# A two-block transformer layer on one core: the first bias strip loaded earlier, the embedding's product by token halves, two silus pinned behind copies

## The chip, the cores and the metric

The kernel runs on one core of a Trainium2 chip. The metric is the device time of one execution in microseconds. Five engines work side by side, each through its own instructions in order: TensorE (PE in the profile, with PEld for its weight loads), VectorE (DVE), ScalarE (ACT), GpSimd (POOL), and SyncE (SP), which here issues the DMAs.

## The reference, cut to what matters

Two transformer blocks over 1024 tokens of width 1024. The change lies in the second block:

```
y_mla  = mla_group(...)        # latent attention, 8 heads: softmax(q k^T) v
y_diff = diff_group(...)       # differential attention, 4 heads, two maps each
x = x + concat(y_mla, y_diff) @ w_out
x = x + conv_ffn(rms_norm(x))  # (silu(conv(h @ w_gate)) * (h @ w_up)) @ w_down
gate = sigmoid(rms_norm(x) @ w_ple_gate)
x = x + gate * (p @ w_ple_proj)

# diff_group, per block of 128 queries
bias   = table[t5_bucket(k_idx - q_idx)]
logits = q k^T * scale + bias, masked by chunks; probs = softmax(logits)
attn   = probs[map 0] - lam * probs[map 1];  lam from lambda_q1, k1, q2, k2
```

## The kernel before

Every fp32 product is made of three products of fp32r halves: a tensor is split into a high part and the rest (names ending in h and l; the weights' halves are both called hl). Weights are loaded as `raw`, then split on ScalarE or GpSimd.

The order of the instructions on each engine is set by a scheduler when the program is built: it goes by its own estimate of when data is ready, and by the order in which the code traces the work. `tc.keep_in_program_order(i)` pins an instruction behind the instruction of the same engine that was traced just before it. Memory is given out in pools that are opened and closed like a stack, on a left and a right side; a tile that falls on a closed pool's memory waits for the readers of what lay there. `bufs` is the number of copies of a tile.

The second block runs like this. `mla()` is the latent attention's loop over head pairs and query blocks. Between its steps `mix` puts pieces of another generator, the fill: `diff_proj()` (the projections of the differential attention), then `ahead()` (its first loads), then `ple_proj()`, the embedding's product p @ w_ple_proj. Then `diff()` is the main loop, with `out2a()` (the first part of the output projection, tiles `mix00` to `mix13`, added into `x`) as its fill.

`ple_proj` transposes nothing: pT, the embedding by columns, is loaded as `p_raw` and split into pT0h, pT0l (tokens 0 to 511) and pT1h, pT1l (512 to 1023). It makes 16 units, one for each of 4 weight groups and 4 token pairs, of 12 matmuls each. A unit's result is copied from PSUM by two ScalarE copies into `p_o` (two buffers) and each is stored to DRAM (`dr_pp`).

`diff()` needs for each head a strip of bias, 128x1024 fp32, loaded from DRAM (`dr_f`) in a skewed view, with one corner set by a GpSimd memset. VectorE adds strip and logits and takes the row's maximum in one instruction (L1341, shown as ISA in the order, CUSTOM_DVE_ANT_0 in the trace), ScalarE takes the exponential, and VectorE joins the two maps with `nlam`, which comes from the small tile `lam` (`lam_p`, `lam_s`).

The feed-forward part, `ffn()`, makes 11 pairs of products: the gate's, and the gated one (h @ w_up) that is multiplied by silu(conv(gate)). Each is made by `wino()`, a two by two block scheme with seven products of 12 matmuls instead of eight, in this order on TensorE: B11, B21, T2, T1, T3, T4, B22 (names of the activations' blocks). Four PSUM tiles are used: x takes B11, T2 and T3 one on top of the other, with copies `u1`, `u2`, `u3` of its state taken by ScalarE (L1571, tile `w_u`) before the next product adds to it; z takes B21, y takes T1 and then B22, q takes T4. In the gated product VectorE adds a copy to a PSUM tile into `f_c` (one buffer, L1621), then multiplies it into `f_y`, silu's output (L1622). It does so in the order z with u1 into the first rows of `ys[0]`, y with u3 into `ys[1]`, q with u3 into `ys[1]`, y with u2 into `ys[0]`. B22 adds to y, so it can't start before the second of these sums has read y. The gated product issues `silu(ys[1])` when u2 is traced, `silu(ys[0])` when u3 is.

Of the kernel before, what the change touches and what calls it, by code (L numbers as in the profile page):

```python
# [11 lines left out]
F32 = mybir.dt.float32  # L12
# [3 lines left out]
AF = mybir.ActivationFunctionType  # L16
ALU = mybir.AluOpType
# [8 lines left out]
NEG = -1e30  # L26
# [138 lines left out]
class Kern:  # L165
# [1099 lines left out]
    def ahead(self):  # L1265

        self.fp_close()
        self.xn2b_close()
        self.qp, self.qp_close = self.open("dfq")
        self.qk0 = self.load_qk(self.qp, self.dr_dqk[0], 0)  # L1270
        yield 0.0

    def diff(self):
        nc, d, tc, vec = self.nc, self.d, self.tc, self.vec
# [5 lines left out]
        sp = es.enter_context(self.pool("df", 1, "right"))  # L1280
# [16 lines left out]
        st, strip = {}, {}  # L1297

        def values(hd, half):
            v = sp.tile([128, 4, 128], F32, tag=f"v{half}", name="v", bufs=2 - half)  # L1300
            nc.sync.dma_start(v, self.dr_dv[:, 4 * half:4 * half + 4, hd * 128:hd * 128 + 128])
            return v

        def first(hd):
            qk = [self.load_qk(qp, self.dr_dqk[hd], 0) if hd else self.qk0]
            o = sp.tile([128, NT, 128], F32, tag="o", name="o", bufs=2)
            skew = self.dr_f[hd][0:1, 127:128]
            strip[hd] = sp.tile([128, 1024], F32, tag="strip", name="strip", bufs=2)
            nc.sync.dma_start(strip[hd], bass.AP(tensor=skew.tensor, offset=skew.offset, ap=[[1152, 128], [1, 1024]]))

            nc.gpsimd.memset(strip[hd][0:64, 960:1024], NEG)
            v = [values(hd, 0)]
            st[hd] = qk, v, o, sp.tile([128, NT], F32, tag="o_ss", name="o_ss", bufs=2)

        def s0(hd, i):
            if i == 0:
                if hd == 0:
                    first(hd)
# [4 lines left out]
            if i == 4 and hd < 3:  # L1323
                first(hd + 1)
# [112 lines left out]
    def ple_proj(self):  # L1437

        nc, d = self.nc, self.d
        with self.pool("pp") as fp:  # L1440
            pT = [self.pair(fp, f"pT{h}", 2) for h in range(2)]
            for h in range(2):
                for k in range(2):
                    pr = fp.tile([128, 512], F32, tag="p_raw", name="p_raw", bufs=1)
                    nc.sync.dma_start(pr, d["pT"][:, k, h * 512:h * 512 + 512])
                    nc.scalar.copy(pT[h][0][:, k], pr)
                    nc.gpsimd.tensor_tensor(pT[h][1][:, k], pr, pT[h][0][:, k].bitcast(F32), ALU.subtract)
            for gi in range(4):
                w = self.W(d["w_pp"][gi])
                for tp in range(4):  # L1450
                    ps = self.tm(w, pT, 2, tp)
                    for j in range(2):
                        o = fp.tile([128, 256], F32, tag="p_o", name="p_o", bufs=2)
                        nc.scalar.copy(o, ps[:, j])
                        nc.sync.dma_start(self.dr_pp[gi, tp, :, j], o)
                    yield 0.25

    def mix_late(self):

# [72 lines left out]
    def wino(self, src, pool, out, ahead=400, then={}):  # L1532
# [5 lines left out]
        with self.tc.high_priority(offset=ahead):  # L1538
            for k in range(2):
                raw = self.wraw.tile([128, 1056], F32, tag="raw", name="raw")[:, :1024].rearrange("p (f n) -> p f n", f=2)  # L1540
                nc.sync.dma_start(raw, src[:, k].rearrange("p f k n -> p f (k n)"))
                raws.append(raw)
            (a11, a21), (a12, a22) = ((r[:, 0], r[:, 1]) for r in raws)

            def split(v):
                hl = self.whl.tile([128, 2, 528], F32R, tag="hl", name="hl")[:, :, :512]
                nc.scalar.copy(hl[:, 0], v)  # L1547
                nc.gpsimd.tensor_tensor(hl[:, 1], v, hl[:, 0].bitcast(F32), ALU.subtract)  # L1548
                return [(hl[:, 0, k * 128:k * 128 + 128], hl[:, 1, k * 128:k * 128 + 128]) for k in range(4)]

            def add(a, b, op):
                v = self.wsum.tile([128, 512], F32, tag="w_s", name="w_s")
                nc.gpsimd.tensor_tensor(v, a, b, op)
                return v
            w1, w2 = split(a11), split(a12)
            s1 = add(a21, a22, ALU.add)
            s2 = add(s1, a11, ALU.subtract)
            w6, w5 = split(s2), split(s1)
            w7 = split(add(a11, a21, ALU.subtract))
            w4 = split(a22)  # L1560
            w3 = split(add(a12, s2, ALU.subtract))
# [30 lines left out]
    def ffn(self):  # L1592

        nc, d, tc, vec = self.nc, self.d, self.tc, self.vec
        with self.pool("ffn", 1) as fp:
            for gi in range(11):
                us = []
                for _ in range(2):
                    u = fp.tile([128, 2 + T], F32, tag="f_u", name="f_u", bufs=2)
                    nc.vector.memset(u[:, 0:2], 0.0)  # L1600
                    us.append(u)

                def gate(ct, half, ps, v):
                    u = us[ct][:, 2 + half * 512:514 + half * 512]
                    nc.vector.tensor_tensor(u, ps, v, ALU.add)  # L1605
                self.wino(d["w_fg"][gi], fp, gate)
                cw = vec["cw2"]
                ys = {}
                for ct in (1, 0):
                    c, u = 2 * gi + ct, us[ct]  # L1610
                    y = fp.tile([128, T], F32, tag="f_y", name="f_y", bufs=2)
                    nc.vector.tensor_scalar(y, u[:, 0:T], cw[:, c, 0:1], vec["cb2"][:, c:c + 1], ALU.mult, ALU.add)  # L1612
                    for j in range(1, 3):
                        nc.vector.scalar_tensor_tensor(y, u[:, j:j + T], cw[:, c, j:j + 1], y, ALU.mult, ALU.add)  # L1614
                    ys[ct] = y
                silu = lambda y: nc.scalar.activation(y, y, AF.Silu)

                def up(ct, half, ps, v):
                    y = ys[ct][:, half * 512:half * 512 + 512]
                    c = fp.tile([128, 512], F32, tag="f_c", name="f_c", bufs=1)  # L1620
                    nc.vector.tensor_tensor(c, ps, v, ALU.add)  # L1621
                    nc.vector.tensor_tensor(y, y, c, ALU.mult)  # L1622
                self.wino(d["w_fu"][gi], fp, up, 400 if gi else 100,
                          {"u2": lambda: silu(ys[1]), "u3": lambda: silu(ys[0])})
                for ct in range(2):
                    nc.sync.dma_start(self.dr_h[2 * gi + ct], ys[ct])
        self.xb_close()
        self.xt_close()
        self.ws_close()
        self.xa_close()  # L1630
# [90 lines left out]
```

## Time and profile before

| what | us |
|---|---|
| median of 3 runs | 2645.79 |
| lowest and highest run | 2638.98, 2645.89 |
| time of the profiled execution | 2637.64 |
| span of the profiled execution | 2635.9 |
| PE busy | 2490.2 (94%) |
| DVE busy | 1435.8 (54%) |
| POOL busy | 1054.8 (40%) |
| ACT busy | 869.3 (33%) |

All times inside the execution count from the span's start. The profiled execution is 8.15 below the median and 1.34 below the lowest of the three runs; its own time is 1.7 over its span. TensorE is busy for most of the span; what it waits for is what a change can win or lose. The mean granted clock of TensorE was 0.982 of full speed.

### The profile page before, as it was taken

What the parts mean: (1) busy time and instruction counts of PE and PEld (TensorE: products, weight loads), DVE (VectorE), ACT (ScalarE), POOL (GpSimd) and SP (SyncE); (2) the same over time, 40 slices, a digit from 0 to 9 for tenths busy, and PEclk for the clock granted to TensorE, in tenths of its full rate; (3) what the DMA queues carried; (4) which work ended last, traced back from release to release, by engine and by line L of the source; (5) the groups of instructions that cost most, each with busy time, mean ns of one, the idle gap of its engine ahead of it and who ended that gap; (6) DMA issues with size and microseconds to landing.
All of it is one profiled execution on the core that took longest, in us unless ns stands there. A gap on an engine that the chain in (4) does not pass through costs nothing.

```text
span 2635.9 us, 38621 instructions
## 1 busy us (share of the span) xinstructions
PE 2490.2 (94%) x15170; PEld 2119.0 (80%) x15170; DVE 1435.8 (54%) x2677; ACT 869.3 (33%) x1599; POOL 1054.8 (40%) x914
## 2 busy tenths in 40 slices
PE   6999999999999999998899989988999999999999
PEld 6888999876777779988787868887777777777789
DVE  5565555275666553368854338846544544433372
ACT  3322223163444341123334346624333333100030
POOL 1524332122122245544533322224777777533322
PEclk9999999999999999999999999989999999999999
DMA  4433223253422455322675457451222122523222
GB/s 163 141 110 112 81 89 105 65 151 97 116 84 69 167 177 180 115 72 90 203 214 167 120 186 205 136 188 58 67 92 80 64 89 87 185 79 104 72 85 93
DMA packets 158766, 313.55 MB, mean 119 GB/s; under 512 B 14804, under 2 KB 62164, under 8 KB 158456
## 3 DMA queue, kind: packets, MB, share of 16 engines
q1 hardware_dynamic: 158584, 311.07, 37.8%
q8 instruction: 120, 1.97, 0.3%
q14 instruction: 62, 0.51, 0.1%
HBM read 214.01 MB, written 100.42 MB: 119 GB/s over the span
## 4 chain that ended last, share of the span: by engine, by line
PE 40%; DVE 9%; DMA 3%; issue 2%; ACT 2%; POOL 1%; SPq 0%; ACTq 0%; DVEq 0%; POOLq 0%
PE pj L1567 13%; PE pj L266 6%; PE pj L264 6%; PE pj L265 6%; DVE f_y L1614 1%; PE po L932 1%; PE pt L925 1%; PE po L1367 1%; DVE f_y L1612 1%; PE z L1337 1%; PE z L264 1%; DVE rs_a L304 1%; PE z L265 1%; PE z L266 1%; DMA f_y<-dr_h 1%
## 5 line engine op out<-in xcount | busy, mean ns | idle before, releaser
L255 POOL TENSOR_SCALAR hl<-raw 128x512 fp32r<-128x512 f32 (+2 forms) x262 | 192.7, 740 | 897.4 <-PE pj L266 884.1
L256 POOL TENSOR_TENSOR hl<-raw,hl 128x512 fp32r<-128x512 f32 (+3 forms) x270 | 367.7, 1369 | 34.0 <-ACT hl L253 17.9
L265 PE MATMUL pj<-hl,xn_0h 128*128 128x256 f32 (+2 forms) x544 | 159.0, 292 | 2.7 <-POOL hl L256 2.7
L264 PE MATMUL pj<-hl,xn_0h 128*128 128x256 f32 (+2 forms) x544 | 160.4, 295 | 0.6 <-DVE qb_st L314 0.6
L264 PE MATMUL pj<-hl,xn_1h 128*128 128x256 f32 (+2 forms) x544 | 159.6, 293 | 0.0
L266 PE MATMUL pj<-hl,xn_0l 128*128 128x256 f32 (+2 forms) x544 | 159.3, 293 | 0.0
L265 PE MATMUL pj<-hl,xn_1h 128*128 128x256 f32 (+2 forms) x544 | 157.3, 289 | 0.0
L266 PE MATMUL pj<-hl,xn_1l 128*128 128x256 f32 (+2 forms) x544 | 157.2, 289 | 0.0
L1548 POOL TENSOR_TENSOR hl<-w_s,hl 128x512 fp32r<-128x512 f32 x88 | 117.6, 1341 | 66.9 <-ACT hl L1547 66.7
L266 PE MATMUL pj<-hl,f_hl 128*128 128x512 f32 x352 | 139.8, 399 | 2.3 <-DVE f_hl L1653 2.3
L264 PE MATMUL pj<-hl,f_hh 128*128 128x512 f32 x352 | 139.7, 397 | 2.0 <-DVE xres L1662 1.6
L1548 POOL TENSOR_TENSOR hl<-raw,hl 128x512 fp32r<-128x512 f32 x66 | 103.1, 1568 | 91.5 <-ACT hl L1547 91.5
L265 PE MATMUL pj<-hl,f_hh 128*128 128x512 f32 x352 | 138.9, 395 | 0.0
L1662 DVE TENSOR_TENSOR xres<-xres,pj 128x512 f32<-128x512 f32 x96 | 65.2, 686 | 129.9 <-PE pj L266 118.2
L264 PE MATMUL pj<-xn_0h,hl 128*128 128x512 f32 x288 | 117.6, 408 | 0.0
L264 PE MATMUL pj<-xn_1h,hl 128*128 128x512 f32 x288 | 116.6, 405 | 0.0
L927 DVE COPY aT<-pt 128x512 f32<-128x512 f32 (+1 forms) x112 | 70.6, 630 | 83.6 <-PE pt L925 83.4
L265 PE MATMUL pj<-xn_1l,hl 128*128 128x512 f32 x288 | 116.1, 403 | 0.0
L266 PE MATMUL pj<-xn_0h,hl 128*128 128x512 f32 x288 | 115.1, 400 | 0.0
L265 PE MATMUL pj<-xn_0l,hl 128*128 128x512 f32 x288 | 114.8, 398 | 0.0
L266 PE MATMUL pj<-xn_1h,hl 128*128 128x512 f32 x288 | 114.4, 397 | 0.0
L1605 DVE TENSOR_TENSOR f_u<-pj,w_u 128x512 f32<-128x512 f32 x44 | 30.3, 689 | 148.6 <-ACT w_u L1571 96.5
(595 smaller groups left out, 7316.9 us busy)
## 6 DMA issues: line engine op xcount, KB each, us to landing
raw<-in_w_o_dram SPq DMA_DIRECT2D x28, 512.0 KB
qk<-dr_mla SPq DMA_DIRECT2D x32, 416.0 KB
dr_mla<-l_st SPq DMA_DIRECT2D x32, 384.0 KB
raw<-in_w_fg_dram SPq DMA_DIRECT2D x22, 512.0 KB
raw<-in_w_fu_dram SPq DMA_DIRECT2D x22, 512.0 KB
dr_h<-f_y SPq DMA_DIRECT2D x22, 512.0 KB
raw<-in_w_fd_dram SPq DMA_DIRECT2D x22, 512.0 KB
f_y<-dr_h SPq DMA_DIRECT2D x22, 512.0 KB
```

What stands on the lines that cost most here:

```text
L255: nc.gpsimd.tensor_scalar(hl[:, 0], raw[:, k:k + c], 1.0, 1.0, ALU.mult, ALU.mult)
L256: nc.gpsimd.tensor_tensor(hl[:, 1], raw[:, k:k + c], hl[:, 0].bitcast(F32), ALU.subtract)
L264: mm(ps, lh[0], rh[0], start=first, stop=False)
L265: mm(ps, lh[0], rh[1], start=False, stop=False)
L266: mm(ps, lh[1], rh[0], start=False, stop=last)
L304: nc.vector.tensor_tensor(a, y, y, ALU.mult)
L925: nc.tensor.transpose(pt[:, b, :], e[a][:, j * 128:j * 128 + 128], self.ident)
L927: copy[j0 // 2 % 2](aT[:, :n], pt[:, :n])
L1548: nc.gpsimd.tensor_tensor(hl[:, 1], v, hl[:, 0].bitcast(F32), ALU.subtract)
L1567: nc.tensor.matmul(ps, w[k][l], b[r][:, k, :], start=first and k + n == 0, stop=k == 3 and n == 2, skip_group_check=not first)
L1605: nc.vector.tensor_tensor(u, ps, v, ALU.add)
L1662: nc.vector.tensor_tensor(xr, xr, ps, ALU.add)
```

## The change

Three edits. First, the strip of head 0 is loaded in `ahead()`, into the pool of the query and key tiles on the left side, right behind the first of these, where before `first(0)` loaded it in `diff()` into `diff`'s own pool; the strips of the later heads come from the same helper and lie in the same pool. Second, `ple_proj` holds all four weight groups and goes through the token halves one after the other, with one pair pTh, pTl that both halves use in turn. Third, the two silus of the gated product are pinned in program order, which puts them behind the copies u2 and u3.

```diff
@@ ahead
         self.qk0 = self.load_qk(self.qp, self.dr_dqk[0], 0)
+        self.strip0 = self.load_strip(0)
         yield 0.0
+
+    def load_strip(self, hd):
+        skew = self.dr_f[hd][0:1, 127:128]
+        strip = self.qp.tile([128, 1024], F32, tag="strip", name="strip", bufs=2)
+        self.nc.sync.dma_start(strip, bass.AP(tensor=skew.tensor, offset=skew.offset, ap=[[1152, 128], [1, 1024]]))
+
+        self.nc.gpsimd.memset(strip[0:64, 960:1024], NEG)
+        return strip
@@ diff, first
-            skew = self.dr_f[hd][0:1, 127:128]
-            strip[hd] = sp.tile([128, 1024], F32, tag="strip", name="strip", bufs=2)
-            nc.sync.dma_start(strip[hd], bass.AP(tensor=skew.tensor, offset=skew.offset, ap=[[1152, 128], [1, 1024]]))
-
-            nc.gpsimd.memset(strip[hd][0:64, 960:1024], NEG)
+            strip[hd] = self.load_strip(hd) if hd else self.strip0
@@ ple_proj
-            pT = [self.pair(fp, f"pT{h}", 2) for h in range(2)]
+            ws = [self.W(d["w_pp"][gi]) for gi in range(4)]
             for h in range(2):
+                pT = self.pair(fp, "pT", 2)
...
+                for gi in range(4):
+                    for tp in range(2 * h, 2 * h + 2):
+                        ps = self.tm(ws[gi], [pT, pT], 2, tp)
...
@@ ffn
-                silu = lambda y: nc.scalar.activation(y, y, AF.Silu)
+                silu = lambda y: tc.keep_in_program_order(nc.scalar.activation(y, y, AF.Silu))
```

At the head of the differential attention, on SyncE, the strip (number 794 is head 0's) stood behind the last stores of the embedding's product (`dr_pp`) and behind `lam`:

```order
L1248 DMA dr_mix<-ob 128x512
L1455 DMA dr_pp<-p_o 128x256
L248 DMA raw<-in_w_o_dram 128x1024
L1455 DMA dr_pp<-p_o 128x256
L1284 DMA lam<-in_lam_dram 128x256
L1455 DMA dr_pp<-p_o 128x256
L1309 DMA strip<-dr_f_794 128x1024
L1301 DMA v<-dr_dv 128x4x128
```

After the change the strip stands 26 rows further ahead, behind the first query loads, and at this place seven of the 32 stores come after `lam`, three of them in these rows:

```order
L1248 DMA dr_mix<-ob 128x512
L1460 DMA dr_pp<-p_o 128x256 x2
L1293 DMA lam<-in_lam_dram 128x256
L1310 DMA v<-dr_dv 128x4x128
L1460 DMA dr_pp<-p_o 128x256
L1405 DMA m_o<-dr_mix 128x512
L1460 DMA dr_pp<-p_o 128x256
L1405 DMA m_o<-dr_mix 128x512
L1310 DMA v<-dr_dv 128x4x128
L1460 DMA dr_pp<-p_o 128x256
```

So the strip has left the queue's end and the stores have moved in behind `lam`. On VectorE at the same place (`ob` is the latent attention's last copy) the work on `lam` came first before the change; now three of the additions with the strip (the ISA rows that name z) stand ahead of it:

```order
L1246 COPY ob<-po 128x128
L1304 TENSOR_SCALAR gdo<-g_do 128x1
L1346 ISA e,a_nm<-z,strip 128x128
L1346 ISA a_nm 128x1
L1347 TENSOR_SCALAR a_nm<-a_nm 128x1
L1346 ISA e,a_nm<-z,strip 128x128
L1346 ISA a_nm 128x1
L1346 ISA e,a_nm<-z,strip 128x256
...
L1355 RECIPROCAL a_r_15225<-a_s 128x1
L1295 TENSOR_TENSOR lam_p<-lam 128x128
```

On TensorE, 36 matmuls of `ple_proj` (three units) now stand behind the latent attention's last product, where before there was none, and between the first token half's last matmul and the second half's first stand nine matmuls and transposes of other work.

In the gated product, on ScalarE (`hl` are the splits of weights for the next product; the three copies are u1, u2 and u3), the silus stood around u1 before the change:

```order
L1616 ACTIVATE f_y<-f_y 128x1024
L1547 CAST hl<-raw 128x512
L1571 COPY w_u_18635<-pj 128x512
L1616 ACTIVATE f_y<-f_y 128x1024
L1547 CAST hl<-w_s 128x512 x2
L1571 COPY w_u_18661<-pj 128x512
L1547 CAST hl<-w_s 128x512
L1547 CAST hl<-raw 128x512
L1571 COPY w_u_18688<-pj 128x512
```

Now the first stands behind u2 and the second behind u3:

```order
L1552 CAST hl<-raw 128x512 x2
L1576 COPY w_u_18635<-pj 128x512
L1552 CAST hl<-w_s 128x512 x2
L1576 COPY w_u_18661<-pj 128x512
L1621 ACTIVATE f_y<-f_y 128x1024
L1552 CAST hl<-w_s 128x512
L1552 CAST hl<-raw 128x512
L1576 COPY w_u_18688<-pj 128x512
L1621 ACTIVATE f_y<-f_y 128x1024
```

No copy waits behind a silu any more. On TensorE the scheduler has moved four matmuls of the next gate product's B11 ahead of the gated product's B22, in all of the first ten pairs:

```order
L1572 MATMUL pj<-T4h,hl 128x512
L1572 MATMUL pj<-B11h,hl 128x512
L1572 MATMUL pj<-B11l,hl 128x512
L1572 MATMUL pj<-B11h,hl 128x512 x2
L1572 MATMUL pj<-B22h,hl 128x512
L1572 MATMUL pj<-B22l,hl 128x512
L1572 MATMUL pj<-B22h,hl 128x512 x2
```

Before, B22 followed T4 directly, and B11 came behind it. VectorE's order in the gated product is the same in both kernels, except in the eleventh pair.

## Rows read from the trace of the kernel before

**Rows 1.** TensorE's waits over the whole span: total us, times, longest.
```profile
PE z L1337 <- DVE a_nm L1341: 16.0, 7, 9.9
PE pj L1567 <- ACT w_u L1571: 10.4, 10, 2.0
```

**Rows 2.** TensorE's timeline at the head of the differential attention: start, duration, idle before.
```profile
1565.01 0.28 PE L265 MATMUL pj<-hl,pT1h 128*128 128x256 f32 x1
...
1566.19 0.28 PE L266 MATMUL pj<-hl,pT1l 128*128 128x256 f32 x1
...
1576.96 0.47 PE L1337 MATMUL z<-k,q 128*128 128x128 f32 x1 [9.91 <-DVE a_nm L1341]
```

**Rows 3.** Timelines of VectorE and of SyncE's queue at the same place.
```profile
1573.92 0.29 DVE L1286 TENSOR_TENSOR lam_p<-lam 128x128 f32<-128x128 f32 x1 [6.48 <-DMA lam<-in_lam_dram]
...
1576.60 0.29 DVE L1341 CUSTOM_DVE_ANT_0 e<-z,strip 128x128 f32<-128x128 f32 x1 [1.40 <-POOL strip L1311]
...
1579.04 0.17 DVE L1350 RECIPROCAL a_r<-a_s 128x1 f32<-128x1 f32 x1 [0.44 <-ACT e L1344]
...
1569.50 0.35 SPq L1284 DMA_DIRECT2D lam<-in_lam_dram  x1
...
1570.96 0.32 SPq L1309 DMA_DIRECT2D strip<-dr_f  x1
```

**Rows 4.** The 32 copies into p_o: what ScalarE waited for ahead of them (us, times).
```profile
  DMA dr_pp<-p_o: 12.5, 10
```

**Rows 5.** Timelines: a load of p_raw, its split on ScalarE, the rest on GpSimd.
```profile
1515.37 0.34 SPq L1445 DMA_DIRECT2D p_raw<-in_pT_dram  x1
...
1518.31 0.62 ACT L1446 CAST pT1h<-p_raw 128x512 fp32r<-128x512 f32 x1 [1.14 <-DMA p_raw<-in_pT_dram]
...
1519.01 1.28 POOL L1447 TENSOR_TENSOR pT1l<-p_raw,pT1h 128x512 fp32r<-128x512 f32 x1 [2.30 <-ACT pT1h L1446]
```

**Rows 6.** Busy time by engine in two stretches, then PEclk, DMA share, GB/s.
```profile
1577.00:1587.00 10.00, 8.74 (x30) 6.99 (x31) 7.19 (x35) 6.25 (x23) 0.00 (x0) 0.58 0.63 238
...
1850.00:1870.00 20.00, 17.98 (x71) 14.14 (x70) 9.74 (x13) 8.96 (x13) 13.07 (x10) 0.91 0.17 53
```

**Rows 7.** TensorE's timeline: a gated product from B11 (1888.62), then a gate product (1909.31).
```profile
1888.62 0.40 PE L1567 MATMUL pj<-B11h,hl 128*128 128x512 f32 x1
...
1895.31 0.50 PE L1567 MATMUL pj<-T2h,hl 128*128 128x512 f32 x1 [0.96 <-ACT w_u L1571]
...
1909.31 0.40 PE L1567 MATMUL pj<-B11h,hl 128*128 128x512 f32 x1
...
1914.89 0.40 PE L1567 MATMUL pj<-T2h,hl 128*128 128x512 f32 x1
...
1926.03 0.40 PE L1567 MATMUL pj<-B22h,hl 128*128 128x512 f32 x1
```

**Rows 8.** ScalarE's timeline: a silu of the gated product, u3 of the gate product.
```profile
1897.50 1.06 ACT L1616 ACTIVATE f_y<-f_y 128x1024 f32<-128x1024 f32 x1 [2.24 <-DVE f_y L1614]
...
1924.04 0.58 ACT L1571 COPY w_u<-pj 128x512 f32<-128x512 f32 x1
```

**Rows 9.** Timelines of VectorE and GpSimd in the same two products.
```profile
1898.59 0.69 DVE L1622 TENSOR_TENSOR f_y<-f_y,f_c 128x512 f32<-128x512 f32 x1 [0.32 <-ACT f_y L1616]
1905.14 0.69 DVE L1621 TENSOR_TENSOR f_c<-pj,w_u 128x512 f32<-128x512 f32 x1 [5.86 <-ACT w_u L1571]
1905.87 1.72 DVE L1622 TENSOR_TENSOR f_y<-f_y,f_c 128x512 f32<-128x512 f32 x1
...
1905.76 1.28 POOL L1553 TENSOR_TENSOR w_s<-w_s,raw 128x512 f32<-128x512 f32 x1
...
1925.26 1.29 POOL L1548 TENSOR_TENSOR hl<-raw,hl 128x512 fp32r<-128x512 f32 x1
```

**Rows 10.** TensorE's timeline in the eleventh gated product: the start of B22.
```profile
2270.19 0.50 PE L1567 MATMUL pj<-B22h,hl 128*128 128x512 f32 x1 [3.28 <-DVE f_c L1621]
```

More of the change, by code (lines that the diff above doesn't have):

```diff
@@ L1445, in ple_proj @@
                     nc.sync.dma_start(pr, d["pT"][:, k, h * 512:h * 512 + 512])
[L1446 to L1456, printed above, removed]
+                    nc.scalar.copy(pT[0][:, k], pr)
+                    nc.gpsimd.tensor_tensor(pT[1][:, k], pr, pT[0][:, k].bitcast(F32), ALU.subtract)
+                for gi in range(4):
+                    for tp in range(2 * h, 2 * h + 2):
+                        ps = self.tm(ws[gi], [pT, pT], 2, tp)
+                        for j in range(2):
+                            o = fp.tile([128, 256], F32, tag="p_o", name="p_o", bufs=2)
+                            nc.scalar.copy(o, ps[:, j])
+                            nc.sync.dma_start(self.dr_pp[gi, tp, :, j], o)
+                        yield 0.25
     def mix_late(self):
```

## The prediction

> **What bounds the kernel now.** I read the page's busy shares first: TensorE works for 94% of the span and the next engine for 54%, so time can come only from TensorE's idle stretches and from its clock. Next I read the view of waits for TensorE, at the two places that the edits touch [rows 1]. At the head of the differential attention seven waits for VectorE's row maximum sum to 16.0 us, and one of them is 9.9. In the feed-forward part ten waits for the copy w_u sum to 10.4, the longest 2.0. Then I read the timelines around both.
>
> At the head, TensorE runs out of work when `ple_proj` and the latent attention end, and its next product starts at 1576.96 after 9.91 idle [rows 2]. It needs VectorE's first addition with the strip, which starts at 1576.60. That one waited for GpSimd's memset of the strip's corner, the memset waited for the strip's load, and the load was issued only at 1570.96, at the end of SyncE's queue and behind `lam` at 1569.50 [rows 3]. VectorE itself had been free since 1573.92 - 6.48 = 1567.44. So here the chain is queue, load, memset, addition, and not work.
>
> In a gated product T2 follows B21 on the tile x, and may start only when u1 is copied out. A silu of 1.06 us stands ahead of that copy on ScalarE [rows 8]. T2 starts 1895.31 - 1888.62 = 6.69 after B11, and in a gate product, which has no silu at this place, 1914.89 - 1909.31 = 5.58 [rows 7]. The silu costs a pair 1.11 us, of which 0.96 is seen as the wait.
>
> **The strip.** It removes no work: the same load and memset go some 26 rows ahead in the queue. The first addition can start when VectorE is free, 1567.44 for 1576.60: **-9.2**. The load's space is free earlier than that, so I expect no new wait for it. What is late next is `lam`. It took at most 1573.92 - 1569.50 = 4.42 from its issue to its first reader. VectorE reached its work on `a_r` 1579.04 - 1576.60 = 2.44 after the first addition [rows 3], and `lam_p` now stands just behind that. If `lam` is issued at about the time of the first addition, VectorE waits 4.4 + 0.2 - 2.4 = 2.2 there, and the additions of the next blocks and so TensorE's next products are queued behind. The moved stores are the second thing: three units of `ple_proj` now stand between the last product of the latent attention and the new one, with six copies into `p_o` on ScalarE among the first exponentials. `p_o` has two buffers; before, ten of 32 copies waited for a store, 12.5 us together, 1.25 each [rows 4]. Three such waits are 3.75. The two run side by side in part: I take **+3.5**, with bounds 2.2 (`lam` alone) and 6.0 (both in a row).
>
> **The embedding's product by halves.** The number of matmuls stays. The 36 that move behind the latent attention are worth (1566.19 - 1565.01) / 10 = 0.118 us each [rows 2], where ten matmuls lie between those two rows: 4.2 us by which the attention can end earlier. Against that stands the single pair of pT. The second half's first split may overwrite it only after the first half's last matmul: a cast of 0.62 and a rest of 1.28, then the second `p_raw` (one buffer) is loaded, 1518.31 - 1515.37 = 2.94, cast and subtracted again [rows 5]: 0.62 + 1.28 + 2.94 + 0.62 + 1.28 = 6.7. Nine other matmuls and transposes stand there, at 0.28 to 0.47 [rows 2] some 3.3 us, and six matmuls of the part that is split first, 0.7. The stall is about 6.7 - 4.0 = 2.7, so the sum of this edit is **-1.5**; bounds -4.2 (stall covered) and +2.5 (nothing covers it).
>
> **The clock at the head.** After the idle stretch TensorE was granted the lower of its two levels, 1.2 GHz, for part of the time: from 1577 to 1587 the mean is 0.58 of full speed, with 8.74 us busy [rows 6]. At 2.4 GHz the same work takes 8.74 x 0.42 = 3.7 less. With a shorter idle stretch some of this comes back; the waits for `lam` and the stores may bring the level down as well. I take half, **-1.8**, with bounds -3.7 and 0. The head sums to -9.2 + 3.5 - 1.5 - 1.8 = -9.0, with bounds -14.9 and -0.7.
>
> **The silus.** In each pair T2 gains 1.11. But `silu(ys[0])` now follows u3, and u3 ends late: in the gate product next to it 1924.04 + 0.58 - 1909.31 = 15.3 after B11 [rows 7, 8]. With the silu of 1.06 it is 16.3 [rows 8]. Only then can VectorE multiply u1's sum into `ys[0]`, and as `f_c` has one buffer, the sum of y and u3 stands behind this multiply, and B22 behind that sum. The sum is 0.69; the multiply is 0.69 alone [rows 9]. TensorE gets to B22 1926.03 - 1909.31 = 16.7 after B11 [rows 7], plus the four B11 matmuls that now stand ahead of it, 4 x 16.72 / 72 = 0.93: 17.65. If the multiply ran alone it would end at 17.0, the sum at 17.7, and B22 would wait 0.05. It may not run alone. In the gate product GpSimd is in an instruction from 1925.26 for 1.29, 15.95 to 17.24 after B11, and where such a multiply met a GpSimd instruction (1905.76 for 1.28) it took 1.72 and ended 0.55 after that one [rows 9]. So I let it end at 17.24 + 0.55 = 17.8, the sum at 18.5, and B22 waits 0.9. Nine pairs then gain 1.11 - 0.9 = 0.2 each: -1.9.
>
> That figure hangs on how the two engines get in each other's way, and the row says: the multiply waits for the whole instruction. The Trainium skill ("SBUF — State Buffer", section "SBUF: two separate sides") says why: VectorE and GpSimd share a pair of ports, and a VectorE operation with two SBUF inputs and a GpSimd operation that reads SBUF hold it one at a time, for the whole instruction. It speaks against this edit, since it moves the multiply from a time when GpSimd was idle to one when it works. By that rule the nine pairs are worth -1.9; without it, 9 x (0.05 - 1.11) = -9.5. The trace of before agrees: 0.69 alone, 1.72 beside GpSimd.
>
> Two pairs differ. In the first, the wait was 2.0 [rows 1], and the granted clock was 0.91 over the 20 us that hold it [rows 6], 1.8 us lost; I take -2.0 - 0.2 - 1.8 + 0.9 = -3.1. In the eleventh no further product stands ahead of B22, which already waits 3.28 for VectorE [rows 10]; the later silu and multiply add 0.7 (the multiply) to 1.7 (blocked too), I take +1.0. The feed-forward part sums to -1.9 - 3.1 + 1.0 = -4.0. Its lower bound is -9.5 - 4.0 + 0.7 = -12.8 (no block). Its upper bound is that the four matmuls don't cover: a wait of 0.9 + 0.93 = 1.8 for 1.11, so 9 x 0.7 - 2.1 + 1.7 = +5.9.
>
> **The sum** is -9.0 - 4.0 = -13.0. Against the profiled execution, 2637.64, it gives 2624.6; that execution is 8.15 under the median of the runs, so against the median it gives 2632.8. I forecast the middle, **2629**.
>
> **The rivals.**
> - GpSimd is out of the way when the multiply comes: the whole feed-forward part then moves against the trace by a microsecond, and GpSimd's instructions with it. The head as above, -9.0 - 12.8 = -21.8: 2615.8 to 2624.0. Against it: GpSimd's row at 1925.26 sits just where the multiply will be, in all pairs alike if the order repeats.
> - The strip's wait is hidden by the next one anyway: `lam`, the stores through two `p_o`, and the single pT pair give back nearly all, the head is worth -1 and not -9. For it: all three wait on DMAs that are issued at about the time when the strip's was, and TensorE's other waits of that group, 16.0 - 9.9 = 6.1 in six [rows 1], may grow. It gives -1 - 4 = -5: 2632.6 to 2640.8, the middle 2637.
> - Slower: the multiply meets two GpSimd instructions in a row. It is then held 1.28 longer [rows 9], the sum ends at 19.8, B22 waits 2.1 in each pair, which is as long as the wait after which the clock fell in the first pair. Nine pairs cost 9 x (2.1 - 1.11 + 1.8) = +25, the other two +2, and with the head's -9 it is +18: 2656 to 2664. It decides from the point where the sum of y and u3 ends later than about 19.6 after B11. Against it: VectorE's request stands first when GpSimd's first instruction ends, and the row at 1905.87 was held by one only.
>
> **How the numbers follow.** Chances: the sum 0.53 (its own range 2619 to 2638), GpSimd out of the way 0.15, the strip replaced 0.24, slower 0.08. Faster or slower counts from 0.3% on, 7.9 us, about what a measurement of this kernel can tell: below 2637.9 or above 2653.7. Of the sum's chance 0.50 lies below, of the strip rival's 0.05, and all 0.15 of the GpSimd case: 0.70 faster, 0.22 within, 0.08 slower. The range 2612 to 2641 leaves out the slower case and the far ends of the two outer rivals.
>
> **What would show it.** At the head, the idle stretch of 9.91 ahead of the first new product is gone or down to a few us, and ended by `lam` or by a store of `dr_pp`, with the granted clock near full speed behind it. TensorE's waits for w_u are gone from the gated product, and new waits of pj for `f_c`, about 0.7 to 0.9, stand in nine or ten pairs; the first multiply of each pair takes some 1.5 us. The clock keeps its level in the first pair, and the eleventh waits longer. At the change of token halves TensorE waits for pTh or pTl. I am wrong if the waits for `f_c` are absent (the block is wrong), if they pass 2 us with a fall of the clock, or if TensorE idles as long at the head, for another tile.

## The result

| kernel | median us | range | runs |
|---|---|---|---|
| before | 2644.97 | 2638.98 to 2645.89 | 4 |
| changed | 2622.61 | 2619.76 to 2628.21 | 4 |

The ratio is 0.9923, with a 95% interval of 0.9904 to 0.9943: 20 us faster, between 15 and 25. The forecast was 2629, in a range of 2612 to 2641. The profiled execution of the changed kernel has a span of 2619.8; the one before had 2635.9.

### The profile page after: what moved, and what is told of

Read it like the earlier page. It is cut to its first block, busy times and chain, and to the rows that moved or that the text cites. A ratio compares the mean times of both kernels' runs of the same rounds, so it can differ in the third digit from the quotient of the medians.

```text
span 2619.8 us, 38637 instructions
## 1 busy us (share of the span) xinstructions
PE 2491.3 (95%) x15170; PEld 2117.2 (81%) x15170; DVE 1437.3 (55%) x2677; ACT 868.6 (33%) x1599; POOL 1078.2 (41%) x914
## 4 chain that ended last, share of the span: by engine, by line
PE 42%; DVE 7%; DMA 3%; ACT 2%; issue 2%; POOL 1%; SPq 0%; DVEq 0%; ACTq 0%; POOLq 0%
PE pj L1572 16%; PE pj L264 6%; PE pj L266 6%; PE pj L265 6%; PE po L932 1%; PE pt L925 1%; DMA qk<-dr_mla 1%; PE po L1372 1%; DVE e L1346 1%; PE z L265 1%; DVE rs_a L304 1%; PE z L264 1%; DMA f_y<-dr_h 1%; PE z L266 1%; PE pt L354 0%
## 5 line engine op out<-in xcount | busy, mean ns | idle before, releaser
L256 POOL TENSOR_TENSOR hl<-raw,hl 128x512 fp32r<-128x512 f32 (+3 forms) x270 | 366.6, 1364 | 33.8 <-ACT hl L253 17.7
L1553 POOL TENSOR_TENSOR hl<-w_s,hl 128x512 fp32r<-128x512 f32 x88 | 131.5, 1495 | 56.9 <-ACT hl L1552 56.5
L1553 POOL TENSOR_TENSOR hl<-raw,hl 128x512 fp32r<-128x512 f32 x66 | 113.0, 1712 | 64.3 <-ACT hl L1552 63.3
```

What stands on the lines that cost most here:

```text
L256: nc.gpsimd.tensor_tensor(hl[:, 1], raw[:, k:k + c], hl[:, 0].bitcast(F32), ALU.subtract)
```

## The profile after

Most lines of the changed kernel stand five further down: the addition with the strip is L1346, the wino copies w_u are L1576, the two steps of the gated product L1626 and L1627.

TensorE's waits over the whole span, as in [rows 1] (total us, times, longest):

```profile
PE pj L1572 <- DVE f_c L1626: 7.0, 3, 4.7
PE z L1342 <- DVE a_nm L1346: 5.8, 6, 2.3
...
PE pj L264 <- ACT p_o L1459: 2.2, 1, 2.2
...
PE pj L264 <- ACT pTh L1452: 1.7, 1, 1.7
...
PE pj L266 <- POOL pTl L1453: 1.6, 3, 0.8
```

The ten waits for w_u are gone. The waits for the row maximum fell from 16.0 to 5.8, and the 9.9 among them is now 2.3. Three waits for f_c stand where one of 3.3 stood before: 4.7 in the eleventh pair, and two of 1.17 and 1.14. The forecast had seen such a wait in every pair. TensorE's wait for a copy into `p_o` is new, and those for pTh and pTl have grown: for each half of the pair they summed to 0.8 before.

The head, from the timelines of VectorE, SyncE's queue and TensorE, which answer to [rows 2, 3]:

```profile
1571.78 0.29 DVE L1246 COPY ob<-po 128x128 f32<-128x128 f32 x1 [2.72 <-PE po L932]
...
1572.05 0.28 DVE L1346 CUSTOM_DVE_ANT_0 e<-z,strip 128x128 f32<-128x128 f32 x1
...
1579.23 0.29 DVE L1295 TENSOR_TENSOR lam_p<-lam 128x128 f32<-128x128 f32 x1 [2.39 <-DMA lam<-in_lam_dram]
...
1575.21 0.38 SPq L1293 DMA_DIRECT2D lam<-in_lam_dram  x1
...
1575.78 0.39 PE L264 MATMUL pj<-hl,pTh 128*128 128x256 f32 x1 [2.23 <-ACT p_o L1459]
...
1580.24 0.50 PE L1342 MATMUL z<-k,q 128*128 128x512 f32 x1 [2.17 <-DVE a_nm L1346]
```

The first addition follows the latent attention's last copy `ob` at once, where before it came 9.5 us after it. What is late next is what the prediction named: `lam`, 2.39 on VectorE and 2.17 on TensorE, and a store of `p_o`, 2.23.

The granted clock and the busy time in the stretches that answer to [rows 6] (columns as there):

```profile
1573.00:1583.00 10.00, 5.58 (x33) 4.62 (x32) 4.82 (x29) 5.14 (x18) 1.88 (x2) 0.92 0.68 231
1843.00:1863.00 20.00, 19.97 (x87) 15.88 (x86) 11.49 (x14) 9.00 (x13) 18.10 (x12) 1.00 0.24 79
```

Behind the new first product the mean is 0.92 and not 0.58, and in the first pair it is 1.00 and not 0.91.

In the gated products two pairs tell the story. The second pair's (its B11 starts at 1878.07) is like eight of the first ten, the fourth pair's (1956.52) is like the other two. VectorE's first multiply, GpSimd beside it, and B22:

```profile
1894.31 0.69 DVE L1627 TENSOR_TENSOR f_y<-f_y,f_c 128x512 f32<-128x512 f32 x1 [5.60 <-ACT f_y L1621]
...
1893.14 1.30 POOL L1558 TENSOR_TENSOR w_s<-w_s,raw 128x512 f32<-128x512 f32 x1
1894.40 1.76 POOL L1553 TENSOR_TENSOR hl<-raw,hl 128x512 fp32r<-128x512 f32 x1
...
1895.85 0.50 PE L1572 MATMUL pj<-B22h,hl 128*128 128x512 f32 x1
...
1972.82 1.84 DVE L1627 TENSOR_TENSOR f_y<-f_y,f_c 128x512 f32<-128x512 f32 x1 [5.69 <-ACT f_y L1621]
...
1971.56 1.30 POOL L1558 TENSOR_TENSOR w_s<-w_s,raw 128x512 f32<-128x512 f32 x1
1972.82 1.30 POOL L1553 TENSOR_TENSOR hl<-raw,hl 128x512 fp32r<-128x512 f32 x1
...
1975.51 0.50 PE L1572 MATMUL pj<-B22h,hl 128*128 128x512 f32 x1 [1.17 <-DVE f_c L1626]
```

At 1894.31 the multiply starts 0.09 ahead of GpSimd's next instruction. It takes its 0.69, and GpSimd's takes 1.76 instead of 1.30. At 1972.82 both start together in the record: GpSimd keeps its 1.30, the multiply takes 1.84 and ends 0.54 after it, and TensorE waits 1.17. The order of the engines is the same in both pairs, so less than a tenth of a microsecond decides. The eleventh pair (its row is 2255.01, against [rows 10]):

```profile
2255.01 0.79 PE L1572 MATMUL pj<-B22h,hl 128*128 128x512 f32 x1 [4.71 <-DVE f_c L1626]
```

## The experiments

The runs scatter by 6 to 17 us within a kernel, so two measures stand side by side. The first is the ratio to the kernel before on the same chip. The second is the length of two stages in each profiled execution: the head, from the latent attention's first logits (first z of qk) to the feed-forward's first weighted product (pj of B11 and hl), and from there to the end. Kernels whose code agrees in a stage show the scatter of one trace: up to 2.7 us in the feed-forward part, and 7 in the head.

| kernel | ratio | interval | head us | feed-forward to the end us |
|---|---|---|---|---|
| before | 1 | | 473.8 | 812.4 |
| e1 pin alone | 0.9981 | 0.9969 to 0.9992 | 476.8 | 804.2 |
| e2 strip and halves | 0.9952 | 0.9934 to 0.9969 | 465.6 | 810.8 |
| e3 halves alone | 1.0020 | 1.0007 to 1.0033 | 477.3 | 810.6 |
| changed | 0.9923 | 0.9904 to 0.9943 | 466.3 | 803.4 |
| e9 changed again | 0.9933 | 0.9917 to 0.9950 | 461.5 | 806.1 |
| e4 silus swapped | 0.9905 | 0.9884 to 0.9926 | 465.6 | 796.4 |
| e8 two f_c | 0.9900 | 0.9879 to 0.9920 | 468.6 | 796.6 |
| e5 silu later | 0.9957 | 0.9940 to 0.9974 | 466.0 | 810.1 |
| e6 lam early | 0.9964 | 0.9951 to 0.9976 | 469.1 | 804.4 |
| e7 four loads | 0.9933 | 0.9913 to 0.9953 | 462.6 | 804.7 |
| e10 swapped, four loads | 0.9902 | 0.9886 to 0.9919 | 463.4 | 797.1 |
| e11 strip a little earlier | 0.9997 | 0.9982 to 1.0011 | 474.8 | 810.0 |

### One part at a time: e1, e2, e3

e1 is the kernel before with the one line of the pin, e2 the changed kernel without it, e3 the kernel before with `ple_proj` of the changed one.

> The kernel before with the third edit alone: the two silus of the gated product pinned behind the copies u2 and u3. Theory A (the two traces read pair by pair: -0.96 in eight of ten pairs, +0.2 in two, -3 in the first one, +1.4 in the eleventh, and some 1 to 2 back behind it): 8 to 10 us faster than before, TensorE's waits for w_u gone, waits for f_c of about 1.15 in one to three pairs and near 0 in the others. Theory B (the prediction's step: the multiply is blocked by GpSimd in every pair): about 4 us faster, a wait for f_c of 0.7 to 1.2 in all ten pairs.

> The changed kernel without the pin: the early strip and the embedding's product by halves. Theory A (by the landmarks of the two traces, the head is worth what is left of the total): 7 to 8 us faster than before, with TensorE's waits for w_u at 10.4 in ten as before. Theory B (the prediction's sum for the head): about 9 us faster. Rival (the strip's wait is replaced by the next ones, and the total comes from the silus): within 2 us of before.

> The kernel before with the second edit alone: the embedding's product by token halves, the strip still at the end of the queue. Theory A (the halves are the price of the strip's room: pTh, pTl and p_o waits let the latent attention end some 4 us later, and nothing is won): 2 to 5 us slower than before, with the long wait ahead of the first new product still 8 to 10. Theory B (the prediction's step: 4.2 us of matmuls move behind the last product and a stall of 2.7 comes in): 1 to 2 us faster. Then the strip alone is worth the difference to the run with both.

The head's waits in e1 and e3 (TensorE, 1500 to 1700), e1 first:

```profile
PE z L1337 <- DVE a_nm L1341: 15.5, 6, 10.0
```

```profile
PE z L1337 <- DVE a_nm L1341: 14.4, 6, 8.8
PE pj L264 <- ACT pTh L1447: 1.5, 1, 1.5
PE pj L266 <- POOL pTl L1448: 1.2, 4, 0.5
PE pj L264 <- ACT p_o L1454: 1.1, 2, 0.8
```

The pin alone is worth 5.0 us by the ratio (2.1 to 8.2) and 8.2 by its stage. In its trace three of ten pairs lose to GpSimd (1.15 to 1.5) and seven wait 0.03 at most. The waits are those of theory A, the time by the ratio falls short of its 8 to 10 and lies nearer to theory B's 4. Strip and halves together are worth 12.7 (8.2 to 17.4) by the ratio and 8.2 by the stage, so the rival in which the next waits eat up the head's gain falls; by the ratio it is more than either theory had (7 to 9). The halves alone cost 5.3 (1.8 to 8.7): theory A. The long wait stays, and the embedding's product adds waits of its own. The difference of e2 and e3, early strip against late with the halves in both, is 18 us by the ratios and 11.7 by the stage. The early strip with the old product was not tried: the two have no room in memory together.

### Who holds B22: e4, e8, e5

```diff
@@ e4
-                          {"u2": lambda: silu(ys[1]), "u3": lambda: silu(ys[0])})
+                          {"u2": lambda: silu(ys[0]), "u3": lambda: silu(ys[1])})
@@ e8
-                    c = fp.tile([128, 512], F32, tag="f_c", name="f_c", bufs=1)
+                    c = fp.tile([128, 512], F32, tag="f_c", name="f_c", bufs=2)
@@ e5
-                          {"u2": lambda: silu(ys[1]), "u3": lambda: silu(ys[0])})
+                          {"u2": lambda: silu(ys[1]), "u3": lambda: (tc.keep_in_program_order(nc.scalar.copy(fp.tile([128, 1], F32, tag="f_w", name="f_w", bufs=1), vec["cb2"][:, 0:1])), silu(ys[0]))})
```

> The changed kernel with the two silus in the other order: ys[0] behind u2, ys[1] behind u3. Theory A (B22 waits for the sum of y and u3 because f_c has one buffer and the multiply ahead of it needs silu(ys[0])): the first multiply starts near 11 after B11 and not 16.3, the waits for f_c (7.0 in three) go, TensorE no longer takes B11 matmuls ahead of B22, and it is 3 to 6 us faster than the changed kernel. Rival (the time in these pairs is set by weights from GpSimd, and the wait only moves): within 1 us of the changed kernel, with a new wait of about the same size in the two pairs and the eleventh.

> The changed kernel with two buffers of f_c. Theory A (only the one buffer ties the sum of y and u3 to the multiply behind silu(ys[0])): the sum runs ahead of the multiply, B22's waits for f_c in the two pairs go, TensorE takes no B11 matmul ahead, and it is 3 to 6 us faster than the changed kernel, like the swapped silus. Rival (VectorE's order keeps the multiply first, so the second buffer changes nothing): within 1 us.

> The changed kernel with one tiny ScalarE copy (128x1) pinned between u3 and silu(ys[0]), so that the first multiply of each gated product is asked for some 0.2 us later. Theory A (VectorE's multiply and GpSimd's next instruction ask for the shared path at nearly the same time, 16.24 to 16.30 after B11, and the one that starts first holds it to its end): now GpSimd comes first in all ten pairs, each first multiply takes 1.5 to 1.9 us for 0.69, B22 waits 0.8 to 1.2 in all ten, and the kernel is 6 to 10 us slower than the changed one, so 10 to 15 faster than before. Rival (the waits of 1.15 in two pairs come from something else, a weight or a late copy): 0.2 us later means 0.2 us per pair, within 3 us of the changed kernel.

TensorE's waits for f_c over the span in e4, e8 and e5, in this order:

```profile
PE pj L1572 <- DVE f_c L1626: 3.3, 1, 3.3
```

```profile
PE pj L1572 <- DVE f_c L1626: 2.8, 1, 2.8
```

```profile
PE pj L1572 <- DVE f_c L1626: 14.4, 11, 4.8
```

In e4 and e8 only the eleventh pair waits, and the stage is 7 us shorter than in the changed kernel. The ratios, 0.9905 and 0.9900, lie 5 to 9 us below those of the changed kernel's two measurements (0.9923 and e9's 0.9933), with intervals that overlap or nearly touch; the stage and the waits carry the reading. TensorE takes no B11 matmul ahead of B22 any more in either. In the second gated product of e4 (B11 at 1876.16) the first multiply starts 10.96 after B11 and not 16.24, as expected, and the sum that B22 needs starts at 15.28. In that of e8 (B11 at 1878.91) that sum has moved ahead of the multiply (e4 first):

```profile
1887.12 0.69 DVE L1627 TENSOR_TENSOR f_y<-f_y,f_c 128x512 f32<-128x512 f32 x1 [0.32 <-ACT f_y L1621]
1891.44 0.69 DVE L1626 TENSOR_TENSOR f_c<-pj,w_u 128x512 f32<-128x512 f32 x1 [3.63 <-ACT w_u L1576]
```

```profile
1894.19 0.69 DVE L1626 TENSOR_TENSOR f_c<-pj,w_u 128x512 f32<-128x512 f32 x1 [4.65 <-ACT w_u L1576]
1894.91 2.63 DVE L1627 TENSOR_TENSOR f_y<-f_y,f_c 128x512 f32<-128x512 f32 x2
```

So the chain is the one that the prediction drew: silu(ys[0]), multiply, the one buffer, the sum, B22. Breaking it at either end frees B22.

e5 puts the multiply a little later, 0.1 us by the trace. Now all ten pairs lose. The second gated product there:

```profile
1895.10 1.82 DVE L1627 TENSOR_TENSOR f_y<-f_y,f_c 128x512 f32<-128x512 f32 x1 [5.70 <-ACT f_y L1621]
```

```profile
1893.84 1.28 POOL L1558 TENSOR_TENSOR w_s<-w_s,raw 128x512 f32<-128x512 f32 x1
1895.09 1.29 POOL L1553 TENSOR_TENSOR hl<-raw,hl 128x512 fp32r<-128x512 f32 x1
```

GpSimd starts 0.01 ahead, and the multiply ends at 1896.92, 0.54 behind it. B22 waits 0.90 to 1.03 in each of the ten, and with the eleventh's 4.8 that makes the 14.4. The stage is 810.1, as long as without the pin: one small copy takes the pin's whole gain away. The ratio, 0.9957, is what e2 has (0.9952). The ten waits sum to 14.4 - 4.8 = 9.6, the changed kernel's two to 7.0 - 4.7 = 2.3, so 7.3 are lost, against 6.7 by the stage. The rival, 0.2 us a pair, falls. The six traces with this order (changed, e1, e5, e6, e7, e9) hold 60 such starts. In the 28 where the multiply is more than 0.01 ahead of GpSimd's instruction it takes 0.69, in the 20 where it is behind it takes 1.45 to 1.84, and of the 12 between, seven are free and five are held.

### The head's next waits: e6, e7, e11

e6 loads `lam` behind the first strip, into that pool's second strip buffer. e7 replaces the two loads of a half by four of half the width with two buffers, in the same room. e11 is the kernel before with head 0's strip load at a higher priority.

```diff
@@ e6, ahead
+        self.lam0 = self.qp.tile([128, 1024], F32, tag="strip", name="strip", bufs=2)[:, :256].rearrange("p (a b) -> p a b", a=4)
+        self.nc.sync.dma_start(self.lam0, self.d["lam"].partition_broadcast(128))
@@ e7, ple_proj
-                for k in range(2):
-                    pr = fp.tile([128, 512], F32, tag="p_raw", name="p_raw", bufs=1)
+                for k, n in ((0, 0), (1, 0), (0, 256), (1, 256)):
+                    pr = fp.tile([128, 256], F32, tag="p_raw", name="p_raw", bufs=2)
@@ e11, diff, first
+            with tc.high_priority(offset=0 if hd else 600):
                 nc.sync.dma_start(strip[hd], bass.AP(tensor=skew.tensor, offset=skew.offset, ap=[[1152, 128], [1, 1024]]))
```

> The changed kernel with lam loaded right behind the first strip, into the strip's second buffer (the second head's strip is loaded after it). Theory A (lam is what VectorE waits for at the head, 2.39 us, and the product behind it waits 2.17): both waits go, 1 to 3 us faster than the changed kernel. Rival (the stores through two p_o buffers end at the same time, so the wait moves to them): within 1 us of the changed kernel, with TensorE's wait for p_o at 2.2 or more.

> The changed kernel with the embedding's columns of a half loaded in four pieces of 128x256 through two p_raw buffers, where it was two of 128x512 through one: the same room. Theory A (the halves cost time because the second load waits for the only p_raw, and TensorE waits for pTh and pTl, 1.7 and 1.6): these waits fall under 1 us and it is 1 to 4 us faster than the changed kernel. Rival (the halves cost time because the product starts late behind four weight groups and its stores stand behind lam): within 1 us of the changed kernel or slower.

> The kernel before with one thing changed: the load of head 0's strip has a higher priority, so it is issued ahead of lam and of the last two stores, some 1.5 to 2 us earlier; its room and the embedding's product stay. Theory A (the head's wait is the strip's way through the queue, and it ends as much earlier as the load is issued): the wait of 9.9 falls to 7.5 to 8.5, the first addition with the strip starts 1.5 to 2 us sooner after the latent attention's end, and the kernel is 1 to 3 us faster, which its measurement can hardly tell from no change. Rival (lam or the transfer itself holds the head): the wait stays within 0.5 us of 9.9.

In e6 `lam` is there early, and VectorE waits for ScalarE's exponential of it instead, behind the copies into `p_o`; TensorE's waits for `p_o` rise:

```profile
1571.67 0.16 DVE L1301 TENSOR_TENSOR nlam<-lam_s 128x1 f32<-128x1 f32 x1 [3.27 <-ACT lam_s L1298]
```

```profile
PE pj L264 <- ACT p_o L1459: 5.7, 6, 2.4
```

The wait only moved, as the rival said, but the rival had the time within 1 us, and the ratio is worse than the changed kernel's by 8 to 11 us. Its trace shows a head 3 to 8 longer than in the two of the changed kernel, and the profiled execution was the fastest of its twelve, 3.9 below their median; why it is slower by more than that is open.

In e7 the wait for pTh is gone and that for `p_o` falls to 0.5, but that for pTl stays, where theory A had it under 1:

```profile
PE z L1342 <- DVE a_nm L1346: 4.3, 7, 1.3
PE pj L266 <- POOL pTl L1453: 1.7, 3, 1.0
PE pj L264 <- ACT p_o L1459: 0.5, 1, 0.5
```

Its head, 462.6, lies within those of the changed kernel, 466.3 and 461.5, and its ratio is that of e9. A gain of 1 to 4 us can't be told here.

In e11 the strip is issued 1.9 after the start of the attention's last copy into `ob`, where it was 3.9 before, and TensorE's next product waits 8.60 for 9.91:

```profile
1568.17 0.29 DVE L1246 COPY ob<-po 128x128 f32<-128x128 f32 x1 [2.72 <-PE po L932]
...
1576.38 0.29 DVE L1341 CUSTOM_DVE_ANT_0 e<-z,strip 128x128 f32<-128x128 f32 x1 [7.85 <-POOL strip L1311]
...
1570.06 0.40 SPq L1309 DMA_DIRECT2D strip<-dr_f  x1
...
1576.73 0.47 PE L1337 MATMUL z<-k,q 128*128 128x128 f32 x1 [8.60 <-DVE a_nm L1341]
```

The wait got 1.3 shorter, short of the 1.5 to 2 expected, since the way from issue to first use grew from 1576.60 - 1570.96 = 5.64 [rows 3] to 6.32. The rival (within 0.5 of 9.9) falls. The time is the same as before, as expected. A place in the queue alone doesn't do it.

### The changed kernel again, and the best version: e9, e10

> The changed kernel itself once more, on the same chip as the next two: the measure for them. All theories: 18 to 25 us faster than before. The port is asked for within 0.1 us by both engines, so which pairs of the gated product lose it (waits of 1.15 ahead of B22) may differ from the first profile: one to four of ten.

> The changed kernel with the swapped silus and the embedding's loads in four pieces together. Theory A (the two act at different places, each on waits that the other does not touch): the silus' 5 and the loads' 2 to 4 add up, 7 to 9 us faster than the changed kernel on the same chip, no wait for f_c but the eleventh's, waits for pTh and p_o under 1. Rival (the loads' gain was the scatter between executions): no more than the silus' 5.

e9 came out at 17.7 us (13 to 22) faster than before, just under the 18 to 25 expected. Four pairs lose to GpSimd there, where it was two in the first profile. e10 has 0.9902 against 0.9933 on the same chip, medians of 2614.06 and 2622.59: 8.5 us better than the changed kernel. By the number alone that is theory A's 7 to 9, and more than the 5 of the rival. But by the stages all of it lies in the feed-forward part (797.1 for 806.1), and none in the head (463.4 for 461.5), where the four loads act, and e4 without them has 0.9905. So a gain of the loads is not shown. The best that was found is e4, e8 or e10, at 25 to 26 us faster than before, and the runs don't tell these three apart.

## Why the prediction was right

The forecast, 2629, rested on a sum of -13.0 for the profiled execution. The stages of the traces give -16: the head is 465.6 on average in six traces with strip, halves and unaltered head code (changed, e2, e4, e5, e8, e9) against 475.3 in two without (before, e1), -9.7, and the feed-forward part is 804.6 in five with the pin as it is (changed, e1, e6, e7, e9) against 811.0 in four without (before, e2, e3, e11), -6.4. The sum of -9.0 and -4.0 was split between the right places, but it is short: by the ratio the change is worth 20 (15 to 25). The forecast lay 6.4 above the measured 2622.61. That it came so near is in part luck, since terms inside the sum were wrong in both directions:

- **The strip, -9.2: right.** The first addition came 9.55 after the latent attention's end at 1567.05 [rows 2, 3], and 0.31 after it in the changed kernel (1571.74): -9.24.
- **`lam` and the stores, +3.5: right in kind, a little small.** VectorE waited 2.39 for `lam` where 2.2 was forecast. TensorE waited 2.17 for it and 2.23 for `p_o`, one after the other, 4.4 together.
- **The halves, -1.5: wrong in sign.** The attention did not end earlier by the 36 matmuls that moved behind it. From its first logits to its end it took 217.4 to 219.4 with the old product (before, e1, e11), and 218.6 to 222.1 with the halves in seven traces (changed, e2 to e5, e8, e9). Alone they cost 5.3 (1.8 to 8.7). The step that failed put a stall of 2.7 at the change of halves. There TensorE waits 0.30 in the changed kernel; it waits at the product's start, 1.75 for the first pTh, then 0.50 and 0.77 for pTl.

The attention's stretch before and after, then the 10 us behind the first wait for pTh in the changed kernel and in e9 (columns as in [rows 6]):

```profile
1349.65:1567.05 217.40, 211.57 (x1677) 172.12 (x1677) 82.98 (x163) 95.25 (x223) 73.56 (x91) 0.99 0.53 151
```

```profile
1350.20:1571.74 221.54, 212.12 (x1642) 170.00 (x1642) 82.43 (x163) 92.68 (x216) 71.53 (x90) 0.98 0.54 147
1521.47:1531.47 10.00, 8.90 (x64) 6.57 (x64) 3.25 (x8) 2.83 (x6) 4.20 (x4) 0.83 0.37 106
```

```profile
1522.61:1532.61 10.00, 8.73 (x75) 6.83 (x76) 3.45 (x9) 3.06 (x7) 4.31 (x4) 1.00 0.42 116
```

TensorE is idle 9.4 in the attention for 5.8 before, and it is busy as long as before though the matmuls are fewer, at a lower clock. The first wait for pTh goes with that clock: where it is 1.4 to 1.9 (changed, e2, e3, e5, e8) the mean behind it is 0.66 to 0.83, and the attention takes 220.7 to 222.1; where it is 0.56 (e4, e9) the mean is 1.00, and it takes 218.6 to 219.2. That is part of the cost. In e7 and e10, without a long wait for pTh, it still takes 220.0 and 221.4, so the rest isn't settled.

- **The clock at the head, -1.8: too small.** Behind the new first product 5.58 us of work ran at 0.92, 0.4 lost, where 3.7 was lost before [rows 6]. Further gains came at the end of the differential attention, which the prediction didn't look at: from its last addition with a strip to the transposes of x it took 71.4 before and 67.4 after.

The two rows of that stretch, before and after (columns as in [rows 6]):

```profile
1710.30:1781.70 71.40, 63.07 (x477) 61.17 (x475) 35.76 (x75) 15.59 (x33) 19.52 (x16) 0.90 0.48 177
```

```profile
1708.40:1775.80 67.40, 61.11 (x478) 59.30 (x476) 34.94 (x73) 15.91 (x34) 19.87 (x16) 0.95 0.49 180
```

TensorE is idle 6.3 there and not 8.3, and its clock is 0.95 and not 0.90. The nine traces with the early strip take 67.0 to 67.5 there and have shorter waits for mix04 and mix05, the four without it take 70.0 to 71.7: the gain goes with the early strip, and why is open.

- **The silu and T2, -1.11 a pair: right.** T2 starts 5.56 to 5.58 after B11 in every pair, and the wait for w_u is gone.
- **B22's wait of 0.9 in every pair: the mis-sized term.** It is 0.01 to 0.03 in eight pairs and 1.14 and 1.17 in two; by the prediction's own sign (waits that are absent) this part was wrong in the eight. The silu's end was forecast well (16.3 after B11; the multiply starts at 16.24 to 16.30). What failed is that GpSimd is in an instruction "15.95 to 17.24 after B11", taken from the gate product of before: in the changed kernel one ends at 16.33 to 16.39, and the next begins at 16.28 to 16.34 where the multiply was first. (The records of the two overlap by 0.05, and GpSimd's are rough.) So the multiply comes just where one hands over to the next. Pairs without a lost start are 0.9 to 1.0 shorter than before and not 0.2, pairs with one are 0.2 longer. e5 makes the forecast case true by 0.1 us: there B22 waits 0.90 to 1.03, behind five B11 matmuls and not four, and the pairs gain nothing.
- **First pair -3.1 and eleventh +1.0.** The first brought 3.6: its fall of the clock is gone. The eleventh cost 1.4 by the wait (4.71 for 3.28) and 1.1 more because B22 then ran at the lower clock (a mean of 0.50 from its start to the next part, 5.3 us, for 0.65 and 4.2 before): +2.5. Some 1.9 came back just behind it.

Of the rivals, the one with GpSimd out of the way (2615.8 to 2624.0) came nearest to the measured time, but not for its reason: GpSimd was never away, it lost a start by less than 0.1 us in most pairs. The head's rival and the slower one did not happen; e5 shows that the second needed a double block that nothing here produces, since in all ten pairs the multiply ends 0.55 behind one instruction of GpSimd.

## What to carry to other kernels

When a wait hangs on two engines that ask for the same path at nearly the same time, the forecast needs both outcomes with their prices, not the one in the nearest row; and a version that takes the loser off the chain (another buffer, or the other order) is worth more than the average of both: 796.5 us in the stage, where the race gave 803.4, 806.1 and 810.1. Room that is made for an early load has a price of its own: run that part alone. At a place where a queue of small loads feeds one engine, taking away the longest wait uncovers the next two, each 2 us here.

## What was not expected of the hardware

A VectorE multiply of two SBUF tiles and a GpSimd instruction that reads SBUF exclude each other in both directions, and the start decides: 0.69 and 1.76 when VectorE is 0.09 ahead, 1.84 and 1.30 where both start together in the record and GpSimd gets its way. The Trainium skill ("SBUF — State Buffer", section "SBUF: two separate sides") states that whichever starts first gets the shared ports for the whole instruction; these rows agree. What it means for timing was the surprise: with the instructions in the same order, the same kernel lost two pairs in one profile and four in another, and a shift of 0.1 us made a stage 4 to 7 us longer (810.1 against 806.1 and 803.4).
